# A one-core encoder block: buffer rooms of the last bonus and of the up weights, a second queue for four gate loads, block copies on VectorE, two pinned orders

## The chip, the cores and the metric

The kernel runs on one core of a Trainium2 chip. The core has five engines, each with its own instruction queue. TensorE (PE) multiplies matrices; its weight loads are listed apart as PEld. VectorE (DVE) and ScalarE (ACT) work on rows of elements, and GpSimd (POOL) does a few elementwise operations here. SyncE (SP) does no arithmetic and issues most of the DMA transfers; POOL issues some too. The engines wait for each other and for DMA transfers by semaphores.

The time is the device time of one execution in microseconds (us), as the median of several runs. The profile beside it is of one execution. "Span" is the time from its first instruction to its last.

## The reference

The kernel computes one encoder block in float32, for 1024 positions of 1024 channels. Cut to what matters:

```python
h = rms_norm(x, norm_mix)
proj = h @ w_in                                   # q, k, v | rwkv columns | 2 x 1024 gate columns
attn = windowed_gqa(q, k, v, sink)                # blocks of 128, +-128 positions, softmax with a sink
zr = zr + shift_mu * (centred_shift(zr) - zr)
#   rwkv7_time_mix: r, k, v, two directions d of decay w and rate a
#   state = state * w + (state @ a) b^T + v k^T;   y = state @ r       (a scan over 1024 positions, both ways)
y = (y - mean) * rsqrt(var + eps) * lnx_w + lnx_b # per head of 64 channels
bonus = einsum(rh, k_dir, r_k)[..., None] * vh    # sum over the channels of a head and over d, times v
rw = (y + bonus) * (sigmoid(gl) @ g2)
gates = sigmoid(proj[gate columns])
merged = gates[0] * (attn @ w_up_attn) + gates[1] * (rw @ w_up_rwkv)
x = x + merged @ w_out
x = x + square(relu(rms_norm(x) @ w_ff1)) @ w_ff2
x = x + (p @ w_ple) * sigmoid(rms_norm(x) @ w_ple_gate)
```

## The kernel before

**Precision.** Each float32 operand of the large products is split in two: `split` (lines 196 to 204) casts it on ACT to a matmul type ("hi", line 198), and one subtraction on DVE or POOL makes the rest ("lo", line 199). Each product is then three matmuls, hi by hi, lo by hi and hi by lo (lines 227, 229, 231; 239 to 241 in another helper). So a weight tile goes through a chain before PE can use it: a DMA of 256 KB into a staging tile `wst`, a cast on ACT, a subtraction.

**Rooms.** Tiles come from pools; a tag with `bufs=2` is two rooms that its tiles take in turn. A tile may be written when all that read the former tile of its room is done. Tiles of another pool that has been closed give their bytes to later pools, and there too the new tile waits for the last reader or writer of the old one, even if that is a DMA.

**What sets the order.** A scheduler orders the instructions of each engine by priority and by its own estimates, before the kernel runs. Some are pinned: matmuls of `mmo` and vector instructions of `turn` stay as the program writes them, and `after(x, y)` puts x behind y. On the chip each engine's queue, and each DMA-issuing queue, is worked through in this fixed order: an instruction that waits holds all behind it on the same queue.

**Stages, in the times of the profiled execution.** Up to about 130 us: the first norm and the q, k, v projections. Up to about 280: for four pairs of RWKV heads p = 0 to 3, projections, the two directions (`kd`, `bk`, `ra` and others, written to DRAM for the scan), and the bonus (`add_bonus`, lines 623 to 642): DVE makes the product rk, PE sums it over a head (`px`, lines 619 and 620), PE turns v (`vtp`, line 633) and ACT copies it to `vt`, SP writes `vt` to `v_d`, and DVE multiplies the sum with v into `bv` (line 638), which SP writes to `bv_d`. From about 280 on PE does the gate columns (`gates`, lines 321 to 333, PSUM tile `gmm`; loop m = 0 to 15 over blocks of 128 columns, halves h of 512 positions) while DVE and ACT finish pair 3. Gate m of half 0 needs its weights through `load_w` (lines 206 to 217), two parts of 256 KB each.

336 to 466 us: the attention, eight tiles n of 128 positions. Per tile: scores `sc` on PE (line 934), softmax on DVE and ACT, transposes (`pt`, line 955), the product with v (`po`, line 963) and its way to DRAM. What is left of the gate matmuls of half 0, and gate 0 of half 1, has the lowest priority and fills in between. Beside it runs the inverse of the first block of scan chunks: `low_products` (lines 791 to 816) loads chunk rows `la` and `lb`, multiplies them on PE (`lps`, line 813), and ACT copies them to `lt` (line 815); it does four chunks (NB = 4), all behind tile n = LOW_AT = 3. Then ACT copies the diagonal 32 x 32 blocks to `Lc` (line 823), and DVE inverts them from tile 5 on in about 31 steps (lines 833 and 836) between its softmax work.

481 to 780 us: the scan, 16 steps of 64 positions in each direction (`qps`, `wa`, `ups`, `sps` and so on), pinned in program order. Between a step's matmuls a generator `beside` (line 986) gives PE fill work: the rest of the gates of half 1, then the attention's up-projection (`uaps`) with weights `wust`, split to `wuhi` and `wulo`, and with the activations `gm`, split to `aTh` and `aTl`. For blocks b = 1, 2, 3 of four chunks the inverse is made in the same loop, one block ahead: `low` (line 1272) copies each chunk's diagonal blocks from `lt` to `Lc` on ACT (line 1279, four copies of 32 x 256 elements a chunk, 48 in all), and `inverse_steps` (line 1281) starts on DVE with the transpose `Lp` (line 1285).

735 to 811 us: the two epilogues (group norm: Ln at line 1103, Square at 1109, Exp at 1119 on ACT, with `rwh` and `rwl` as the split results). 811 to 860: the RWKV up-projection (`mmc`, `mmo`), gate by gate: a gate tile `g1t` is loaded from DRAM, DVE scales and adds it, and the sum is split into `mh` and `ml`, which the output projection reads with the weights `wo0h`, `wo0l`. From 860: output projection, norms, the two feed-forward products (`ff1ps`, `ff2ps`) and the last embedding, up to 1684.

## Time and profile before

| what | value |
|---|---|
| median of 3 runs | 1685.11 us (1683.96 to 1685.51) |
| the profiled execution's own time | 1685.89 us |
| its span | 1684.1 us |
| mean granted TensorE clock over the span | 0.986 |
| busy share of the span: PE, DVE, ACT, POOL | 96%, 67%, 50%, 6% |
| 285 to 300 us: span 15.00, PE busy | 10.39 us |
| 330 to 340 us: span 10.00, PE busy | 5.70 us |
| 396 to 420 us: span 24.00, PE busy | 21.10 us |
| 485 to 520 us: span 35.00, PE busy | 31.31 us |
| 690 to 735 us: span 45.00, PE busy | 39.77 us |
| 735 to 811 us: span 76.00, PE busy | 68.35 us |

How the rows are read: a row of the timeline gives the start, the duration, the engine, the source line, the operation, "output<-input", the shape, the count, and in brackets the idle time of the engine just before it with what ended it. Matmul rows overlap, since the next one starts before the former has drained; the chain of waits ("critical") gives them without the overlap. A row of a window gives the busy time of each engine in that stretch, the granted clock (PEclk, 1.00 is full), the busy share of the 16 DMA engines and the GB/s. SPq is SP's issue queue; "DMA x" in the chain is the time until a transfer landed.

### The profile page before, as it was taken

Reading aid. Unit: us, or ns where it says so; the run is one execution under the profiler, and the core shown is the slowest. Engines: PE = TensorE matmul, PEld = TensorE weight load, DVE = VectorE, ACT = ScalarE, POOL = GpSimd, SP = SyncE. Lnnn points to the kernel's source line nnn. Section 1 sums busy time; section 2 is a strip of 40 time slices with the busy share of each in tenths; the row PEclk is TensorE's granted clock in tenths of the full one; section 3 lists DMA queues with packets and bytes.
Section 4 is the critical chain, followed back from the end, with each engine's and each line's share of the span. In section 5 each row is a group of like instructions: output and inputs, shape, how many; then the busy total and the mean of one; then the engine's idle time right before and its main releaser. Section 6 shows DMA issues by size and latency. Waiting matters only on the chain.

```text
span 1684.1 us, 31165 instructions
## 1 busy us (share of the span) xinstructions
PE 1615.9 (96%) x12280; PEld 1307.8 (78%) x12280; DVE 1134.6 (67%) x2055; ACT 844.5 (50%) x1535; POOL 103.1 (6%) x113
## 2 busy tenths in 40 slices
PE   7999998899999999898999999999999999999998
PEld 7987776776677787676778788888888888888887
DVE  5648998265947596777744876667667877685342
ACT  5557887367744545456313554444435344544121
POOL 3440000221200000000000000000000000000000
PEclk9999999999999999799999999999999999999999
DMA  6353556764286554547652154444449865564110
GB/s 223 82 155 98 171 163 202 227 172 130 88 230 198 139 179 134 163 130 238 207 179 100 57 177 161 144 165 147 138 167 349 273 204 162 164 212 148 38 41 38
DMA packets 200834, 269.23 MB, mean 160 GB/s; under 512 B 47728, under 2 KB 103920, under 8 KB 200688
## 3 DMA queue, kind: packets, MB, share of 16 engines
q1 hardware_dynamic: 190752, 254.14, 47.6%
q0 software_dynamic: 9792, 12.59, 2.9%
q8 instruction: 96, 1.57, 0.4%
q10 hardware_dynamic: 144, 0.52, 0.1%
q14 instruction: 50, 0.41, 0.1%
HBM read 186.45 MB, written 80.74 MB: 159 GB/s over the span
## 4 chain that ended last, share of the span: by engine, by line
PE 74%; DVE 10%; DMA 6%; ACT 5%; issue 3%; POOL 1%; SPq 0%; DVEq 0%; ACTq 0%; POOLq 0%
PE ff2ps L1882 18%; PE ff1ps L1630 16%; PE gmm L221 4%; DMA wst<-in_w_col_dram 2%; PE plps L231 2%; PE plps L229 2%; PE plps L227 2%; PE mm L239 2%; PE mm L240 2%; PE mm L241 2%; PE uaps L221 1%; PE gps L221 1%; PE mmo L241 1%; PE mmo L239 1%; PE mmo L240 1%
## 5 line engine op out<-in xcount | busy, mean ns | idle before, releaser
L1882 PE MATMUL ff2ps<-th,sl 128*128 128x512 f32 x448 | 174.3, 389 | 0.0
L1882 PE MATMUL ff2ps<-tl,sh 128*128 128x512 f32 x448 | 174.3, 389 | 0.0
L1882 PE MATMUL ff2ps<-th,sh 128*128 128x512 f32 x448 | 173.9, 389 | 0.0
L198 ACT CAST sh<-sst 128x512 fp32r<-128x512 f32 x109 | 67.8, 622 | 100.4 <-PE ff2ps L1882 50.9
L199 DVE TENSOR_TENSOR sl<-sst,sh 128x512 fp32r<-128x512 f32 x109 | 75.0, 688 | 44.0 <-ACT sh L198 43.5
L1630 PE MATMUL ff1ps<-mh,w1h 128*128 128x512 f32 x256 | 100.3, 392 | 2.0 <-ACT w1h L198 2.0
L198 ACT CAST whi<-wst 128x512 fp32r<-128x512 f32 x100 | 60.3, 618 | 81.9 <-DMA wst<-in_w_col_dram 30.3
L1630 PE MATMUL ff1ps<-ml,w1h 128*128 128x512 f32 x256 | 99.9, 390 | 0.0
L1630 PE MATMUL ff1ps<-mh,w1l 128*128 128x512 f32 x256 | 99.6, 390 | 0.0
L1882 PEld LDWEIGHTS ff2ps<-tl,sh 128*128 128x128 f32 x448 | 84.1, 188 | 17.7 <-DVE tl L199 0.2
L1882 PEld LDWEIGHTS ff2ps<-th,sh 128*128 128x128 f32 x448 | 84.0, 188 | 17.6 <-ACT th L198 0.3
L1882 PEld LDWEIGHTS ff2ps<-th,sl 128*128 128x128 f32 x448 | 84.1, 188 | 17.5
L183 POOL TENSOR_TENSOR rstd<-ms,neghalf 128x1 f32<-128x1 f32 x24 | 14.5, 606 | 1019.7 <-PE ff2ps L1882 572.3
L198 ACT CAST w1h<-w1st 128x512 fp32r<-128x512 f32 x48 | 28.3, 620 | 96.3 <-DMA w1st<-in_w_ff_dram 59.6
L199 DVE TENSOR_TENSOR wlo<-wst,whi 128x512 fp32r<-128x512 f32 x72 | 47.9, 687 | 29.5 <-ACT whi L198 29.4
L199 DVE TENSOR_TENSOR w1l<-w1st,w1h 128x512 fp32r<-128x512 f32 x48 | 31.7, 687 | 51.6 <-ACT w1h L198 51.6
L227 PE MATMUL gmm<-hh,whi 128*128 128x512 f32 x136 | 57.0, 419 | 4.6 <-ACT whi L198 4.6
L1630 PEld LDWEIGHTS ff1ps<-mh,w1h 128*128 128x128 f32 x256 | 48.1, 188 | 12.9 <-ACT w1h L198 2.8
L231 PE MATMUL gmm<-hh,wlo 128*128 128x512 f32 x136 | 56.8, 419 | 0.0
L1630 PEld LDWEIGHTS ff1ps<-mh,w1l 128*128 128x128 f32 x256 | 48.1, 188 | 10.9 <-DVE w1l L199 0.8
L229 PE MATMUL gmm<-hl,whi 128*128 128x512 f32 x136 | 56.5, 416 | 0.0
L1630 PEld LDWEIGHTS ff1ps<-ml,w1h 128*128 128x128 f32 x256 | 48.1, 188 | 10.0
(405 smaller groups left out, 4530.9 us busy)
## 6 DMA issues: line engine op xcount, KB each, us to landing
wst<-in_w_col_dram SPq DMA_DIRECT2D x92, 256.0 KB, 3.4
tst<-in_w_ff_dram SPq DMA_DIRECT2D x80, 256.0 KB, 4.1
w1st<-in_w_ff_dram SPq DMA_DIRECT2D x32, 512.0 KB, 5.1
hid_S<-h SPq DMA_DIRECT2D x64, 256.0 KB, 2.1
sst<-hid_S SPq DMA_DIRECT2D x64, 256.0 KB, 3.2
hid_A<-h SPq DMA_DIRECT2D x48, 256.0 KB, 2.0
sst<-hid_A SPq DMA_DIRECT2D x45, 256.0 KB, 4.0
ra_d<-ra SPq DMA_DIRECT2D x8, 1024.0 KB, 5.7
```

The costliest lines, as they stand in the source:

```text
L183: nc.gpsimd.tensor_tensor(out=r, in0=ms, in1=neghalf.broadcast_to([P, width]), op=ALU.pow)
L198: a = nc.scalar.copy(hi, src)
L199: b = (lo_eng or nc.vector).tensor_tensor(out=lo, in0=src, in1=hi.bitcast(F32), op=ALU.subtract)
L221: tc.keep_in_program_order(nc.tensor.matmul(*a, **kw))
L227: mm(ps, ah, bh, start=(i == 0), stop=False)
L229: mm(ps, ah, bl, start=False, stop=False)
L231: mm(ps, al, bh, start=False, stop=(i == n - 1))
L239: nc.tensor.matmul(ps, ah, bh, start=(i == 0), stop=False)
L240: nc.tensor.matmul(ps, ah, bl, start=False, stop=False)
L241: nc.tensor.matmul(ps, al, bh, start=False, stop=(i == n - 1))
L1630: nc.tensor.matmul(ps, x_[:, k, :], y_[:, k, :], start=start and k + i == 0, stop=k == 3 and i == 2, skip_group_check=True)
L1882: nc.tensor.matmul(banks[bs][i], x_[:, isl], y_, start=fresh and p + j == 0, stop=p == NPR - 1 and j == 2, skip_group_check=True)
```

## The change

1. The four loads of gates m = 1 and 2 of half 0 (two of 256 KB each) are issued from POOL's queue and not SP's (GQ, and the argument q of `load_w`).
2. `bv` of the last pair takes the room of `kd` and no longer that of `vt`.
3. The low products of the first block are made two chunks behind tile 3 and two behind tile 4 of the attention, where all four stood behind tile 3 (LOW_AT).
4. The 48 copies of diagonal blocks in the scan loop are done by DVE in a pinned place, and each chunk's copies one chunk later: those of chunk ci stand ahead of the low products of chunk ci + 1, the last ones ahead of `Lp`. The 4 copies of the first block (line 823) stay on ACT.
5. In the pool of the up-projection, the weights' staging tile for m = 2 and the first gate tile `gta` are allocated and loaded before `wuhi` and `wulo`, so that these take other bytes of the pool.
6. The Exps of the second epilogue are put behind its last Ln, as those of the first already are (EXPIN). In the instruction list the table loads of ACT in the second epilogue go from four to two.
7. The four casts and four subtractions of the output weights `wo0h`, `wo0l` (128 x 1024 each) are put behind the epilogue's last split. They now stand among the instructions of the RWKV up-projection.

```diff
--- before.py
+++ after.py
@@ -35,7 +35,7 @@
 WOAT = (0, 4)
 
 NFS = {0: "s0 c0", 1: "s1 c1 t0", 2: "s2 c2 t1", 3: "s3 c3 t2", 4: "s4 c4 t3", 5: "s5 c5 p0", 6: "s6 c6 p1", 7: "s7 c7 p2"}
-EXPIN = (1, 0)
+EXPIN = (1, 1)
 EPS_AT = (3, 3, 2, 2)
 VH = 8
 TPAT = (1, 3)
@@ -54,6 +54,7 @@
 FILL0 = 4
 
 GATT = 1
+GQ = ((0, 1), (0, 2))
 
 BRIDGE = 6
 FILL = (5, 5, 3, 5, 3, 2, 4, 1)
@@ -65,7 +66,7 @@
 FILLQ = 8
 TURNS = ((0, 0, 4), (3, 2, 5), (3, 2, 5), (4, 3, 1))
 
-LOW_AT = 3
+LOW_AT = (3, 4)
 INV_AT = 5
 GN_EPS = 64e-5
 W_SCALE = -0.5 * float(np.exp(np.float64(-0.5)))
@@ -193,17 +194,20 @@
 
     on_pool = [None]
 
-    def split(hi, lo, src, lo_eng=None, pin=False):
+    def split(hi, lo, src, lo_eng=None, pin=False, behind=None):
 
         a = nc.scalar.copy(hi, src)
         b = (lo_eng or nc.vector).tensor_tensor(out=lo, in0=src, in1=hi.bitcast(F32), op=ALU.subtract)
+        for x_, y_ in zip((a, b), behind or ()):
+            after(x_, y_)
         if lo_eng is nc.gpsimd:
             on_pool[0] = b
         if pin:
             tc.keep_in_program_order(a)
             tc.keep_in_program_order(b)
-
-    def load_w(pl, tag, src, n, bufs=2, sbufs=2, lo_eng=None, stag=None, parts=1, stages=()):
+        return a, b
+
+    def load_w(pl, tag, src, n, bufs=2, sbufs=2, lo_eng=None, stag=None, parts=1, stages=(), q=None):
 
         k = src.shape[1]
         hi = pl.tile([P, k, n], F32R, name="whi", tag=tag + "_hi", bufs=bufs)
@@ -212,7 +216,7 @@
         for i in range(0, k, step):
             spl, stg, sb = stages[(i // step) % len(stages)] if stages else (pl, stag or tag + "_st", sbufs)
             st = spl.tile([P, step, n], F32, name="wst", tag=stg, bufs=sb)
-            nc.sync.dma_start(st, src[:, i:i + step])
+            (q or nc.sync).dma_start(st, src[:, i:i + step])
             split(hi[:, i:i + step], lo[:, i:i + step], st, lo_eng or nc.gpsimd)
         return hi, lo
 
@@ -322,7 +326,7 @@
 
         for m in ms:
             c0 = O_GATE + m * P
-            hi, lo = load_w(PW, "w", w_col(c0), P, parts=2, lo_eng=lo_of(m))
+            hi, lo = load_w(PW, "w", w_col(c0), P, parts=2, lo_eng=lo_of(m), q=nc.gpsimd if (h, m) in GQ else None)
             ps = PMM.tile([P, 512], F32, name="gmm", tag="mm", bufs=2)
             yield from mm3_steps(ps, [(hi[:, k, :], lo[:, k, :], Hh[h][:, k, :], Hl[h][:, k, :]) for k in range(KT)], mm)
             th = PW.tile([P, 512], F32, name="gth", tag="gth", bufs=2)
@@ -633,7 +637,7 @@
                     nc.tensor.transpose(tp[:, j, :], vz[:, (4 * q + j) * P:(4 * q + j + 1) * P], ident)
                 nc.scalar.copy(vt[:, 4 * q:4 * q + 4, :], tp)
             nc.sync.dma_start(v_d[:, p * P:(p + 1) * P].rearrange("(t q) c -> q t c", q=P), vt)
-            bv = A1.tile([P, T], F32, name="bv", tag="vt", bufs=1)
+            bv = A1.tile([P, T], F32, name="bv", tag="kd" if p == NP - 1 else "vt", bufs=1)
             for hs, ps in next(sums):
                 nc.vector.tensor_tensor(out=bv[:, hs], in0=ps, in1=vz[:, hs], op=ALU.mult)
             for e in range(2):
@@ -969,8 +973,10 @@
                 next(low0)
             if n == 1:
                 zi = zi_tile(BI, "zi")
-            if n == LOW_AT:
-                lts[0] = list(low0)[-1]
+            if n in LOW_AT:
+                for _ in range(NB // len(LOW_AT)):
+                    lts[0] = next(low0)
+            if n == LOW_AT[-1]:
                 for d in range(ND):
                     for a in (load_ra(0, d), load_bk(0, d)):
                         after(a, put)
@@ -1009,10 +1015,18 @@
         aTh = UA.tile([P, NP, 512], F32R, name="aTh", tag="aTh", bufs=1)
         aTl = UA.tile([P, NP, 512], F32R, name="aTl", tag="aTl", bufs=1)
 
+        def gate_of(m, h):
+            g = UA.tile([P, 512], F32, name="gta", tag="g1t", bufs=2)
+            nc.sync.dma_start(g, g_d[m, :, 512 * h:512 * h + 512])
+            return g
+
+        sts.append(load_wu(UA, 2))
+        gta = [gate_of(0, 0)]
+
         def weights(m, st=None):
             hi = UA.tile([P, NP, P], F32R, name="wuhi", tag="wu_hi", bufs=3)
             lo = UA.tile([P, NP, P], F32R, name="wulo", tag="wu_lo", bufs=3)
-            split(hi, lo, st or load_wu(UA, m))
+            split(hi, lo, load_wu(UA, m) if st is None else st)
             return hi, lo
 
         def part(k):
@@ -1030,9 +1044,8 @@
             for m in range(KT):
                 hi, lo = ahead.pop(0)
                 if (h, m) != (0, 0) and (h, m) < (1, KT - 1):
-                    ahead.append(weights((m + 1) % KT))
-                g = UA.tile([P, 512], F32, name="gta", tag="g1t", bufs=2)
-                nc.sync.dma_start(g, g_d[m, :, hs])
+                    ahead.append(weights((m + 1) % KT, sts.pop(2) if sts[2:] else None))
+                g = gta.pop() if gta else gate_of(m, h)
                 ps = PMM.tile([P, 512], F32, name="uaps", tag="mm", bufs=2)
                 for j, _ in enumerate(mm3_steps(ps, [(hi[:, k, :], lo[:, k, :], aTh[:, k, :], aTl[:, k, :]) for k in range(NP)], mmo)):
                     if (h, m) == (0, KT - 1) and j and j % 3 == 0:
@@ -1124,7 +1137,7 @@
             ps = PB.tile([P, 2, 256], F32, name="gps2", tag="gps", bufs=2)
             mm(ps, g2[:, p * P:(p + 1) * P], sge, start=True, stop=True)
             nc.vector.scalar_tensor_tensor(out=rs, in0=rs, scalar=col("lnx_b", p), in1=ps, op0=ALU.add, op1=ALU.mult)
-            split(rwh[:, p, :], rwl[:, p, :], rs.rearrange("q a t -> q (a t)"))
+            epi["done"] = split(rwh[:, p, :], rwl[:, p, :], rs.rearrange("q a t -> q (a t)"))
             yield
 
     AC = [PH0, None]
@@ -1271,15 +1284,22 @@
 
     def low(b, ci):
 
-        lt = lts[b] = next(lows[b])
-        if ci == 0:
+        if ci:
+            diagonal(b, ci - 1)
+        else:
             Lcs[b] = BI.tile([P, 32, 32], F32, name="Lc", tag="inv", bufs=3)
+        lts[b] = next(lows[b])
+
+    def diagonal(b, ci):
+
+        lt = lts[b]
         for r0 in range(0, P, 32):
             k = r0 // 32 % 2
-            nc.scalar.copy(Lcs[b][r0:r0 + 32, 8 * ci:8 * ci + 8], lt[r0:r0 + 32, 8 * ci:8 * ci + 8, 32 * k:32 * k + 32])
+            turn(nc.vector.tensor_copy(Lcs[b][r0:r0 + 32, 8 * ci:8 * ci + 8], lt[r0:r0 + 32, 8 * ci:8 * ci + 8, 32 * k:32 * k + 32]))
 
     def inverse_steps(b):
 
+        diagonal(b, NB - 1)
         Lc = Lcs.pop(b)
         Lp = BI.tile([P, 32, 32], F32, name="Lp", tag="inv", bufs=3)
         turn(nc.vector.transpose(out=Lp, in_=Lc.rearrange("s p t -> s t p")))
@@ -1430,7 +1450,7 @@
         for k in ks:
             st = spl.tile([P, 2, 512], F32, name="wst", tag=tag, bufs=sbufs)
             nc.sync.dma_start(st, wov[:, k:k + 2, 512 * n:512 * n + 512])
-            split(wo[n][0][:, k:k + 2], wo[n][1][:, k:k + 2], st)
+            split(wo[n][0][:, k:k + 2], wo[n][1][:, k:k + 2], st, behind=None if n else epi["done"])
 
     wo_tiles(WO1, 0)
 
```

The following rows are from the instruction lists of the engines, in order, with what an instruction waits for in brackets where that is given.

POOL, between the end of the q and k writes and the loads for the attention (`wst` are gate weights, `qT` and `kT` the attention's operands, `wlo` subtractions for gates). Before:

```order
L754 DMA qT<-qT_d 128x1024
L767 DMA qT<-qT_d 128x1024
L762 DMA kT<-kT_d 128x4x256
L199 TENSOR_TENSOR wlo<-wst,whi 128x512 x2
L762 DMA kT<-kT_d 128x4x256 x2
L199 TENSOR_TENSOR wlo<-wst,whi 128x512 x2
L762 DMA kT<-kT_d 128x4x256
```

After:

```order
L219 DMA wst<-in_w_col_dram 128x512 x2
L758 DMA qT<-qT_d 128x1024
L219 DMA wst<-in_w_col_dram 128x512
L771 DMA qT<-qT_d 128x1024
L219 DMA wst<-in_w_col_dram 128x512
L766 DMA kT<-kT_d 128x4x256
L200 TENSOR_TENSOR wlo<-wst,whi 128x512 x2
L766 DMA kT<-kT_d 128x4x256 x2
```

Three of the four new loads stand ahead of a `qT` load, and all four ahead of the first `kT` load.

DVE, from the end of the last pair to the attention's first softmax (`s2l` and `wlo` are subtractions, `smk` the masked scores). Before:

```order
L199 TENSOR_TENSOR wlo_2871<-wst_2872,whi_2870 128x512 [waits DMAHW5_49,PE_49,Activation_49]
L199 TENSOR_TENSOR wlo_2871<-wst_2876,whi_2870 128x512 [waits DMAHW0_49,Activation_49]
L638 TENSOR_TENSOR bv_3027<-px_3028,z_2693 128x512 [waits DMAHW2_49,DMAHW4_49,PE_49,Activation_49]
L638 TENSOR_TENSOR bv_3027<-px_3031,z_2693 128x512 [waits PE_49]
L917 TENSOR_SCALAR nsink_3060<-band_2922 128x8 [waits DMAHW7_49,DVE_49]
L935 ISA smk_3066,mx_3062<-sc_3067,band_2922 128x256 [waits DMAHW6_49,PE_49]
```

After:

```order
L200 TENSOR_TENSOR s2l_3010<-rk_2595,s2h_3009 128x512 [waits Activation_49]
L200 TENSOR_TENSOR wlo_2871<-wst_2876,whi_2870 128x512 [waits DMAHW2_49,Activation_49]
L642 TENSOR_TENSOR bv_3027<-px_3028,z_2693 128x512 [waits PE_49]
L642 TENSOR_TENSOR bv_3027<-px_3031,z_2693 128x512 [waits PE_49]
L921 TENSOR_SCALAR nsink_3060<-band_2922 128x8 [waits DMAHW3_49,DVE_49]
L939 ISA smk_3066,mx_3062<-sc_3067,band_2922 128x256 [waits PE_49]
```

The first `bv` waited for two DMA queues, PE and ACT; it now waits for PE alone.

ACT, where the up-projection's first weights are cast in the scan (`gth` is the last gate of half 1, `W` belongs to a scan step). Before:

```order
L329 ACTIVATE gth_8291<-gmm_8076 128x512 [waits DMAHW7_49,PE_49,Activation_49]
L1216 COPY W_8368<-wa_8333 128x512 [waits DVE_49,PE_49]
L198 CAST wuhi_8304<-wust_4673 128x512 [waits DMAHW5_49,Activation_49]
L198 CAST aTh_8302<-gm0_4612 128x512 x2
L198 CAST aTh_8302<-gm1_4613 128x512 x2
L198 CAST wuhi_8320<-wust_4675 128x512
```

After:

```order
L333 ACTIVATE gth_8291<-gmm_8076 128x512 [waits DMAHW3_49,PE_49,Activation_49]
L1229 COPY W_8372<-wa_8337 128x512 [waits DVE_49,PE_49]
L199 CAST wuhi_8308<-wust_4673 128x512
L199 CAST aTh_8302<-gm0_4612 128x512 [waits Activation_49]
L199 CAST aTh_8302<-gm0_4612 128x512
L199 CAST aTh_8302<-gm1_4613 128x512 x2
```

The first `wuhi` waited for a DMA queue and for ACT; it now waits for nothing.

## The prediction

> **What bounds the kernel now.** I read the page first, then windows by stage, then the timeline and the chain of waits in the windows that have gaps.
>
> ```profile
> PE 1615.9 (96%) x12280; PEld 1307.8 (78%) x12280; DVE 1134.6 (67%) x2055; ACT 844.5 (50%) x1535; POOL 103.1 (6%) x113
> 285.00:300.00 15.00, 10.39 (x38) 7.86 (x36) 9.38 (x10) 4.21 (x6) 0.76 (x1) 0.77 0.97 304
> 300.00:330.00 30.00, 30.00 (x130) 24.16 (x129) 6.90 (x9) 10.76 (x19) 9.34 (x9) 1.00 0.78 228
> 330.00:340.00 10.00, 5.70 (x21) 4.30 (x21) 2.24 (x7) 1.73 (x3) 3.14 (x3) 0.87 0.76 234
> 396.00:420.00 24.00, 21.10 (x212) 15.09 (x213) 9.30 (x34) 16.38 (x38) 4.14 (x5) 0.93 0.57 155
> 420.00:466.00 46.00, 41.85 (x216) 28.29 (x213) 44.62 (x148) 33.23 (x93) 8.56 (x7) 0.97 0.26 81
> 860.00:960.00 100.00, 99.54 (x464) 81.23 (x463) 59.84 (x90) 37.10 (x63) 5.68 (x8) 1.00 0.28 101
> ```
>
> The columns are span, then PE, PEld, DVE, ACT and POOL busy, the granted clock, the DMA share, and GB/s. PE sets the time: 96% busy over the span, 99.54 of 100 us from 860 on, where nothing changes. So there is nothing to win except PE's gaps and the slow clock behind them, and the change works in windows that have both. The gaps of the windows quoted up to 466 us are 4.6, 0, 4.3, 2.9 and 4.2 us.
>
> **Part 1, gate loads on POOL's queue.**
>
> ```profile
> 280.44 4.16 SPq L640 DMA_DIRECT2D bv_d<-bv  x2
> 284.69 8.75 DMA wst<-in_w_col_dram
> 279.62 0.56 POOL L754 DMA_DIRECT2D qT<-qT_d  x1 [162.43 <-PE px L221]
> 294.14 0.80 PE L227 MATMUL gmm<-hh,whi 128*128 128x512 f32 x1 [4.61 <-ACT whi L198]
> 298.67 0.43 PE gmm L227
> 301.09 0.23 PE gmm L229
> wst<-in_w_col_dram SPq DMA_DIRECT2D x92, 256.0 KB, 3.4
> ```
>
> SP was held from 280.44 to 284.6 by the writes of an earlier `bv`; only then did it issue the next gate's weights, which took 8.75 us to land against a median of 3.4, with the DMA engines 0.97 busy. PE idled 4.61 us and then ran some 13 matmuls at 0.43 in place of 0.23, that is 13 x 0.20 = 2.6 us. POOL was issuing a load at 279.62, so its queue could have issued these weights about 5 us earlier (284.69 - 279.62), more than the 4.61 us missing. Ceiling 7.2 us. Floor: the bytes in flight are the same, and if the DMA engines and not the queue set the 8.75 us, the start 5 us earlier still brings something; floor 2. I take 5.2, nearer the ceiling, because SP's hold (4.2 us) alone is nearly the 4.61 missing. All four loads come ahead of the first `kT` on POOL, whose loads begin at 279.62; the scores that need it come at 336.40, so even 20 us of delay there are free.
>
> The Trainium skill, "Trainium Kernel Development and Optimization", section Key Constraints, says that DMAs of SP, ACT and POOL run on the same 16 DMA engines and that issuing from several only saves the sequencer's issue time. Read strictly this is worth only SP's own hold: 284.69 - 280.44 = 4.2 us earlier, about 4 us of the 7.2. It does not speak of the case here, where a queue stands behind an instruction that waits. The sum goes by the rows.
>
> **Part 2, room of the last `bv`.**
>
> ```profile
> 327.03 0.39 PE L620 MATMUL px<-s2l,one_r 128*128 128x512 f32 x1
> 331.02 4.50 DMA v_d<-vt
> 335.65 1.29 DVE L638 TENSOR_TENSOR bv<-px,z 128x512 f32<-128x512 f32 x2 [22.38 <-DMA v_d<-vt]
> 336.40 0.74 PE L934 MATMUL sc<-kT,qT 128*128 128x256 f32 x4 [4.30 <-DVE bv L638]
> 339.86 0.43 PE gmm L229
> ```
>
> The sums `px` are there at 327.4, but `bv` stands until 335.65, until the write of `vt` to DRAM has landed, because it takes that room. The scores wait 4.30 us for it, since they take the PSUM rooms of `px`. In the new list `bv` waits for PE alone. Its new room, `kd`, was last read when rk was made, which is ahead of `px` in any case. The scores can start about 327.4 + 0.7 + 0.1 = 328.2. Gained: the gap 4.30 and 8 matmuls at 0.43 (8 x 0.20 = 1.6 us), 5.9 us. `bv_d` is written earlier, which nobody waits for before the epilogue. Gate matmuls that stood ahead of the scores (15 fewer in the new PE list before the first one) move behind them; they are fill work and lose nothing as long as their weights are there. Bounds: 7 with what later reading gives, and 3 if the weights of the gates are the next to be late (DMA share 0.76 to 0.78). I take 6.
>
> **Part 3, low products in two halves.**
>
> ```profile
> 403.39 4.88 DMA lb<-bk_d
> 408.36 0.30 PE L813 MATMUL lps<-lb,la 64*64 64x64 f32 x2 [2.54 <-DMA lb<-bk_d]
> 396.38 2.79 PE L963 MATMUL po<-pT,V 128*64 128x512 f32 x12
> 419.38 2.80 PE L963 MATMUL po<-pT,V 128*64 128x512 f32 x12 [0.24 <-ACT pT L959]
> ```
>
> Products of four chunks in a row behind tile 3 use up their loaded rows; the third waits 2.54 us for a load, then, as behind the other gaps, a few matmuls run slow (six would be 1.2 us). Tile 3 to tile 4 takes 23.0 us (419.38 - 396.38). With two chunks, a tile, and two more, the loads of chunks 2 and 3 have a tile's time. Gain up to 2.54 + 1.2 + 2 for the smoother tile = 6; nothing if the inverse on DVE (44.62 of 46 us busy from 420 to 466) is what ends the stage, since `Lp` then starts no earlier. `Lc` stays on ACT there. I take 4: parts 1 and 2 bring everything earlier by the same amount, and the start of `Lp` with them. The attention stage gets 28 gate matmuls less (6.5 us) and its tail 28 more; the tail waits for the end of the inverse on DVE anyway. I book 0 for that: it may cost 3 if the weights of these 28 come late, half of their 6.5, or win 2 of the 4.2 that PE idles from 420 to 466.
>
> **Part 4, diagonal copies on DVE.**
>
> ```profile
> 498.10 1.65 ACT L1279 COPY Lc<-lt 32x256 f32<-32x256 f32 x4
> 507.72 0.33 PE L221 MATMUL lps<-lb,la 64*64 64x64 f32 x2 [1.66 <-ACT lt L815]
> 510.99 0.32 PE L221 MATMUL lps<-lb,la 64*64 64x64 f32 x2 [1.41 <-ACT lt L815]
> 515.28 2.04 DVE L1285 STREAM_TRANSPOSE Lp<-Lc 128x1024 f32<-128x1024 f32 x1 [5.96 <-ACT Lc L1279]
> 706.28 0.68 DVE L864 COPY zi<-Zn 32x1024 f32<-32x1024 f32 x1
> 520.00:552.00 32.00, 31.97 (x691) 26.08 (x689) 30.66 (x78) 13.58 (x26) 0.00 (x0) 1.00 0.64 181
> ```
>
> On ACT four copies take 1.65 us and stand between a chunk's `lt` and the next; PE waits 1.66 and 1.41 us for `lt` here, and DVE 5.96 us for the last `Lc`. DVE copies 1024 elements on 32 partitions in 0.68 us; no row has 256. Bounds for one: 0.68 x 256/1024 = 0.17, and ACT's 0.41. I take 0.25, nearer the scaled one, so 48 copies are 12 us on DVE, 36 of them in a place where it waits anyway. PE wins up to 1.66 + 1.41 at step 0, and a little at steps 4 and 8; but where the inverse runs DVE is 30.66 of 32 us busy, and PE's gap there is 0.03. I take 3 (0 to 5).
>
> **Part 5, rooms of the up weights.**
>
> ```profile
> 684.72 4.11 DMA g_d<-gth
> 688.91 0.62 ACT L198 CAST wuhi<-wust 128x512 fp32r<-128x512 f32 x1 [2.85 <-DMA g_d<-gth]
> 689.56 0.69 DVE L199 TENSOR_TENSOR wulo<-wust,wuhi 128x512 fp32r<-128x512 f32 x1 [4.14 <-ACT wuhi L198]
> 690.10 0.80 PE L221 MATMUL uaps<-aTh,wuhi 128*128 128x512 f32 x1 [3.74 <-ACT aTh L198]
> 704.64 3.62 PE L221 MATMUL qps<-Zn,lt 32*32 32x32 f32 x128 [4.30 <-DVE Zn L1300]
> ```
>
> `wuhi` takes bytes of a gate tile `gth` whose write to DRAM lands at 688.83. In the new list it waits for nothing and can follow ACT's instruction before it, 2.85 us earlier, which is ACT's idle time in the row. PE's first gap shrinks by that; DVE, which stands 4.14 us, goes on with the inverse as much earlier, and the second gap ends with DVE's `Zn`. So the stretch from 686 to 704.64 gets 2.85 us shorter, and part of the slow clock goes: eight `uaps` at 0.43 (1.6 us). I take 4 (2 to 6).
>
> **Parts 6 and 7, epilogue and output weights.**
>
> ```profile
> 788.37 1.28 ACT L1103 ACT_TABLE_LOAD   x1
> 794.54 1.28 ACT L1119 ACT_TABLE_LOAD   x1
> 792.51 0.50 PE L221 MATMUL mups<-rwh,one_r 128*128 128x512 f32 x1 [2.38 <-ACT rwh L198]
> 790.25 1.04 ACT L198 CAST wo0h<-wst 128x1024 fp32r<-128x1024 f32 x1
> 791.32 1.23 DVE L199 TENSOR_TENSOR wo0l<-wst,wo0h 128x1024 fp32r<-128x1024 f32 x1 [0.52 <-ACT wo0h L198]
> 855.68 0.50 PE L239 MATMUL mmo<-wo0h,mh 128*128 128x512 f32 x1 [1.25 <-ACT mh L198]
> ```
>
> Two of four table loads go (2 x 1.28 = 2.56 us of ACT), and a cast of 1.04 leaves the chain that ends with PE's wait of 2.38 us: 3 us there. The casts come back in the RWKV up-projection: 4 x 1.04 on ACT and 4 x 1.23 on DVE, in the queue ahead of `mh` and `ml`. That stage's chain goes through DVE and ACT and PE waits 1.25 us at its end. Price: 0 if they fit where DVE waits for loads, up to 4.9 of DVE. I take 1.5, so +1.5 (-2 to +3.5) for both.
>
> The Trainium skill, "ScalarE: Activation LUTs", section What ACT_TABLE_LOAD costs, gives about 2.66 us for a switch, of which 1.28 is the load and the rest a drain; by that two would be 5.3 us of ACT. The rows agree on 1.28. They show no drain of that size: 788.37 + 2.66 would be 791.03, and ACT casts at 790.25. The sum goes by 1.28.
>
> **Sum.** 5.2 + 6 + 4 + 0 + 3 + 4 + 1.5 = 23.7 us. The profiled execution took 1685.89 (span 1684.1 and 1.8 around it): 1662.2. The median, 1685.11, lies 0.8 below it, so 1661.4; I say 1662.
>
> **The rivals.**
>
> *The gates' weights become the bound in place of the waits removed.* For: DMA share 0.97 and 0.78 from 285 to 330. With both gaps gone PE asks 7 us earlier for the later gates' weights, and two staging rooms give a gate's load, cast and subtraction (3.4, the median, + 0.62 + 0.69, the rows of the same shape in part 5 = 4.7 us for each half) little more time than its 24 matmuls take (24 x 0.23 = 5.5). Against: 30.00 of 30 us busy from 300 to 330 with the same loop. It would leave 2 of part 1, 3 of part 2, and 2 of part 3: 2 + 3 + 2 + 3 + 4 + 1.5 = 15.5, so 1670.
>
> *DVE becomes the bound.* For: DVE 97% busy from 420 to 466 and 96% from 520 to 552. Then part 3 gives 0, part 4 costs 3 (12 of its copies at 0.25 inside the busy stretches), and the moved subtractions cost 2 more than booked: 23.7 - 4 - 6 - 2 = 11.7, so 1674.
>
> *Slower: SP's queue holds the scan.* The new early loads of part 5 (`wust` for m = 2 and `gta`) need rooms of a pool that opens late. If these rooms come free late, SP stands with the loads of `la`, `lb` and the scan rows behind it. Price of one such hold: a load's 4.88 us plus the slow clock behind it, 2.6, so 7.5 us a step. It makes the kernel slower from the fourth step on (4 x 7.5 = 30, over 23.7 + 3.4): 1692. Against: both loads stand at one place of the queue, ahead of the first `wuhi`, so one hold is likelier than four.
>
> *The change doesn't do what it says in the rooms.* Bytes of parts 2 and 5 could wait for another late transfer. The lists show no DMA wait at either instruction, so only a PE or ACT wait can remain. It would take 6 + 4: 1672.
>
> **How the numbers follow.** Forecast 0.60; weights 0.17; DVE 0.10; rooms 0.05; slower 0.04; all gains near their ceilings 0.04 (7.2 + 7 + 6 + 2 + 5 + 6 + 3.5 = 36.7, so 1649). About 0.2% (3.4 us) is the least that a measurement of this kernel can tell from no change. Faster by more than that holds in all but the slower rival and in the tails of the DVE and weights cases, which take 0.04: faster 0.90, same 0.05, slower 0.05. The likeliest case alone spans 1655 to 1669; the range reaches down half way to the ceilings and up beyond the DVE case, 1652 to 1679.
>
> **What would show it.** Right: no PE gap over 1 us from 285 to 300 and from 327 to 337; `bv` within 1.5 us of the last `px`; `lps` with no wait for a load; the first `uaps` within 1 us of `W`; two table loads in the second epilogue. Wrong: `gmm` waiting for `whi` in new places (weights), `qps` or `lps` waiting for DVE more than before (DVE), `la` or `lb` late at several steps (SP's queue), or PE gaps of over 2 us each ahead of `mmo` (output weights).

## The result, and where the time went

| | kernel before | changed kernel | ratio, 95% interval |
|---|---|---|---|
| first session, median | 1685.28 us (8 runs, 1683.4 to 1687.87) | 1676.01 us (8 runs, 1670.11 to 1681.76) | 0.9944 [0.9923, 0.9965] |
| another session, median | 1684.68 us (12 runs) | 1675.65 us (7 runs) | 0.9944 [0.9924, 0.9965] |

The change makes the kernel 9.3 us faster (0.56%). The forecast was 1662, some 23 us faster, with a range of 1652 to 1679. The way was right and the range holds the time, but the gain is well under half of what was forecast; that the range reached up to the time was for the sake of another case (DVE as the bound), and its holding is luck. Single runs of either kernel spread by some 10 us (the changed kernel's over 11.7 in the first session, those of the kernel before over 9.8 in the other); the last section comes back to that.

The profiled execution of the changed kernel took 1677.74 us, span 1676.0, to be held against 1685.89 and 1684.1. Its windows, with the columns as in the prediction:

```profile
285.00:300.00 15.00, 13.72 (x58) 10.39 (x58) 10.71 (x12) 8.56 (x12) 1.31 (x2) 1.00 0.89 292
300.00:330.00 30.00, 27.46 (x116) 21.55 (x115) 9.64 (x16) 9.05 (x16) 9.86 (x9) 0.94 0.88 250
330.00:340.00 10.00, 8.45 (x44) 6.61 (x42) 3.97 (x20) 4.98 (x18) 6.30 (x6) 1.00 0.97 292
396.00:420.00 24.00, 23.47 (x178) 16.20 (x180) 16.99 (x60) 22.13 (x59) 1.70 (x3) 1.00 0.43 126
466.00:485.00 19.00, 10.48 (x172) 8.69 (x163) 2.91 (x5) 5.23 (x9) 0.00 (x0) 0.64 0.85 251
```

The gaps that the prediction spoke of have shrunk: 1.3 us from 285 to 300 (4.6 before), 1.6 from 330 to 340 (4.3), 0.5 from 396 to 420 (2.9). From 300 to 330, where PE had no gap, it now has one of 2.5. The last row is new. The same window of the kernel before was nearly full:

```profile
466.00:485.00 19.00, 17.76 (x251) 12.85 (x248) 9.91 (x14) 6.65 (x12) 0.00 (x0) 0.97 0.93 257
```

So PE lost 8.5 us and a third of its clock at the place where the attention ends and the scan begins. The starts of a few matmuls, read from PE's timeline, turn this into a ledger. The second profile of the changed kernel is from the other session.

| PE starts | before | changed | changed, second profile | gained since the row above (before minus changed) |
|---|---|---|---|---|
| last `px` | 327.03 | 325.34 | 325.79 | 1.7 |
| first `po` (tile 0) | 357.96 | 347.61 | 347.70 | 8.7, of which 4.0 are 17 gate matmuls moved behind |
| last `po` (tile 7) | 465.62 | 449.41 | 449.50 | 5.9, of which 2.6 are 11 more gate matmuls |
| first `qps` | 481.29 | 479.67 | 479.08 | -14.6, of which 6.6 are these 28 gate matmuls |
| `qps` of the third block inverse | 704.64 | 696.58 | 691.13 | 6.4 |
| first `mmc` | 802.32 | 792.34 | 786.95 | 1.9 |
| first `mmo` | 849.47 | 841.41 | 835.00 | -1.9 |
| end of the span | 1684.1 | 1676.0 | 1669.2 | 0.0 |

Without the moved matmuls (0.235 us each) the stages up to the attention's end gained 9.6 us, its tail lost 8.0, the scan gained 6.4, and the rest nothing. The scan's figure is that of one execution: by the second profile it gained 11.3 (212.05 us from the first `qps` to that of the third inverse, against 216.91 and 223.35). Here is the tail in the changed kernel, SP's timeline first:

```profile
454.35 0.33 SPq L219 DMA_DIRECT2D wst<-in_w_col_dram  x1
461.67 1.63 SPq L797 DMA_DIRECT2D la<-ra_d  x1
465.42 1.99 SPq L1001 DMA_DIRECT2D gm<-at_d  x4
467.46 0.91 SPq L1005 DMA_DIRECT2D wust<-in_w_up_attn_dram  x2
468.46 0.85 SPq L219 DMA_DIRECT2D wst<-in_w_col_dram  x2
```

Then its chain of waits, DVE and PE (the `gm` on DVE is the scan's masked product; the `gm` that SP loads is the attention's activation):

```profile
468.46 5.72 DMA wst<-in_w_col_dram
474.85 0.69 DVE L200 TENSOR_TENSOR wlo<-wst,whi 128x512 fp32r<-128x512 f32 x1 [9.37 <-ACT whi L199]
475.46 1.02 DVE L1181 TENSOR_TENSOR gm<-gps,gmask 128x384 f32<-128x384 f32 x2
476.07 1.97 PE L1198 MATMUL tmps<-ident,bkc 128*128 128x128 f32 x8 [8.52 <-DVE gm L1181]
```

Gate m = 1 of the second half needs two weight loads. SP issued the first at 454.35. The second stands behind 22 other loads, sixteen for the scan, four `gm` and two `wust`, and left at 468.46. SP's rows show it issuing these for some 12 of the 14.1 us, so the queue was busy rather than held by a wait. On DVE the subtraction `wlo` that needs it stands ahead of the mask product `gm`, and PE's `tmps` waits for that. One late load thus held three queues. In the kernel before, both loads of this gate (457.90) and both of the next (469.54) stood ahead of the scan's loads on SP:

```profile
457.90 1.71 SPq L215 DMA_DIRECT2D wst<-in_w_col_dram  x2
469.54 1.06 SPq L215 DMA_DIRECT2D wst<-in_w_col_dram  x2
471.14 0.95 SPq L898 DMA_DIRECT2D bkc<-bk_d  x2
477.06 1.35 PE L221 MATMUL gps<-rac,bkc 64*64 64x128 f32 x32 [1.21 <-DVE gm L1168]
```

The gap there was 1.21 us, by the same path and behind the later pair, so the pattern could have been read before the change. Why the scheduler, which orders by its own estimates, placed the loads differently in the changed kernel is not shown.

### The profile page after: what moved, and what is told of

The parts are those of the page before. It is cut to its first block, busy times and chain, and to the rows that moved or that the text cites. A ratio compares the mean times of both kernels' runs of the same rounds, so it can differ in the third digit from the quotient of the medians.

```text
span 1676.0 us, 31183 instructions
## 1 busy us (share of the span) xinstructions
PE 1611.0 (96%) x12280; PEld 1305.8 (78%) x12280; DVE 1156.0 (69%) x2103; ACT 821.1 (49%) x1485; POOL 105.4 (6%) x117
## 4 chain that ended last, share of the span: by engine, by line
PE 71%; DVE 13%; DMA 7%; ACT 3%; issue 3%; SPq 1%; POOL 1%; DVEq 0%; POOLq 0%; ACTq 0%
PE ff2ps L1902 18%; PE ff1ps L1650 16%; DMA wst<-in_w_col_dram 3%; PE gmm L225 2%; PE mm L243 2%; PE mm L244 2%; PE mm L245 2%; PE plps L235 2%; PE plps L233 2%; PE plps L231 2%; DMA g1t<-g_d 2%; DVE tmp L1313 1%; DVE Z L1316 1%; PE qps L225 1%; PE mmo L245 1%
```

## The experiments

All times are medians; the ratio is to the kernel before, run in the same session on the same chip (1682.3 to 1684.7 in these sessions). As base for the single parts serves the first experiment, in which the tail's wait is gone, so that a part's worth is not hidden by it. "Above the base" compares medians of different sessions, between which the kernel before moved by up to 2.4 us.

**The tail's weights on another queue.** One edit to the changed kernel:

```diff
-GQ = ((0, 1), (0, 2))
+GQ = ((0, 1), (0, 2), (1, 1))
```

> The changed kernel, and besides it the two weight loads of gate m = 1 of the second half go by GpSimd's queue. The first gap of the scan in the changed kernel is 8.52 us ahead of tmps (476.07); DVE stands on a wlo there, whose weights SP issued at 468.46 behind la, lb, gm and wust. Theory A (SP's queue makes them late): they leave at about 455, the gap ahead of tmps falls below 1.5 us, the slow clock behind it goes (about 4 us), time 1663 to 1667. Theory B (the DMA engines are full there, 0.81 to 0.86 busy, and the bytes cannot come sooner): the gap stays over 5 us, time 1673 to 1678.

Measured: 1669.67 us, ratio 0.9918 [0.9891, 0.9944]. POOL's timeline and PE's `tmps`:

```profile
453.74 0.57 POOL L219 DMA_DIRECT2D wst<-in_w_col_dram  x1 [0.30 <-POOL wlo L200]
455.95 0.56 POOL L219 DMA_DIRECT2D wst<-in_w_col_dram  x1 [0.30 <-POOL wlo L200]
466.93 1.03 PE L1198 MATMUL tmps<-ident,bkc 128*128 128x128 f32 x8
```

The second load leaves 12.5 us earlier (455.95 against 468.46), `tmps` runs without a wait, and the first `qps` comes at 468.82 against 479.67. The DMA engines were not the limit. Theory A holds at the place, but the time stays above its 1663 to 1667: of the 10.9 us gained there it shows some 6, as the repetition in one session confirms:

> The changed kernel itself, beside the next two runs on the same chip. 8 to 11 us faster than the kernel before; the gap ahead of the first tmps 7 to 9 us.

> The changed kernel with the loads of the second half's gate m = 1 on GpSimd's queue, again. Theory A (the wait at the start of the scan and the slow clock behind it cost the changed kernel its 8 to 11 us of landmark, of which later stages keep more than half): 4 to 8 us faster than the changed kernel in the same session. Theory B (the later stages take it back, since the inverse on DVE sets the end of the third block): within 2 us of it.

Measured: the changed kernel 1675.65 us, 0.9944 [0.9924, 0.9965], its gap ahead of `tmps` 8.15; with the edit 1669.35 us, 0.9921 [0.9894, 0.9949]. The medians differ by 6.3 us. The intervals still overlap, so the time alone would not prove the edit; the wait that is gone in both profiles does. Some of the gain is given back between the third inverse's `qps` and the first `mmc`, which takes 95.8 us in both profiles of the changed kernel and 100.9 and 97.6 with the edit; why stays open.

**The first three parts alone, and the other four alone.** Made from the changed kernel by setting the other parts back: the first with ACT's copies, the old order in the up-projection's pool, EXPIN = (1, 0) and no `behind`; the second with

```diff
-GQ = ((0, 1), (0, 2))
+GQ = ()
-LOW_AT = (3, 4)
+LOW_AT = (3,)
-            bv = A1.tile([P, T], F32, name="bv", tag="kd" if p == NP - 1 else "vt", bufs=1)
+            bv = A1.tile([P, T], F32, name="bv", tag="vt", bufs=1)
```

> Parts 1, 2 and 3 alone (gate loads on POOL, room of bv, low products in two halves); parts 4 to 7 as before. Theory A (what the attention wins is given back at the start of the scan): the last po comes at 449 to 451, qps at 479 to 481, and the slow clock behind the gap costs 3 to 4 us more: 1682 to 1688, no gain. Theory B (the loss sits in parts 4 to 7): the 9 us that the attention wins are kept, 1674 to 1677.

> Parts 4 to 7 alone; parts 1 to 3 as before, so the attention and the start of the scan are as before (qps at 481). Theory A: the scan wins 6.4 us and the 3.7 that the slow clock took in the changed kernel, the epilogue and the RWKV up-projection cancel: 1673 to 1677. Theory B (parts 4 to 7 lose, parts 1 to 3 win): 1682 to 1687.

Measured: parts 1 to 3 alone 1680.68 us, 0.9985 [0.9969, 1.0002]; parts 4 to 7 alone 1679.48 us, 0.9975 [0.996, 0.999]. Theory A is right on the first by its places (last `po` at 449.37, a wait of 8.79 us ahead of `tmps`, `qps` at 479.90), though the time is 1.3 us under its range. On the second the gain is 3 to 4 us, less than theory A said and not the loss of theory B. The profiles hold a surprise. From the first `qps` to that of the third inverse the kernel before took 223.35 us, parts 4 to 7 alone 217.24 (698.02 - 480.78), and parts 1 to 3 alone 216.12 (696.02 - 479.90), though they change nothing in the scan. ACT's rows of parts 1 to 3 alone tell why:

```profile
679.53 0.59 ACT L1228 COPY W<-wa 128x512 f32<-128x512 f32 x1 [0.73 <-PE wa L225]
680.01 0.62 ACT L199 CAST wuhi<-wust 128x512 fp32r<-128x512 f32 x1
```

`wuhi` follows `W` at once, where in the kernel before it waited 2.85 us for the write of the last gate. In the instruction list with parts 1 to 3 (not shown here) it waits for the write of the gate before the last: which of two rooms the last gate takes has flipped. So the removal of this wait, which was to be the gain of part 5, came with parts 1 to 3 as well, and was counted once too often.

**Part 1 undone on the base**, GQ = ((1, 1),):

> As the run with the two loads of the second half on GpSimd's queue, but without part 1 (the four loads of the first half are back on SP's queue). Theory A (the weights are bound by bytes and by two staging rooms there, so the queue is worth little: px moved by 1.7 us): 1 to 2.5 us slower than with part 1. Theory B (part 1 is worth the 5.2 us that the prediction gave it): 4.5 to 6 us slower.

Measured: 1671.9 us, 0.9927 [0.9901, 0.9954], 2.2 us above the base, in theory A's range, though the two intervals overlap. PE's gap is back, while with part 1 the changed kernel has two smaller ones. The row of this experiment:

```profile
293.20 0.80 PE L231 MATMUL gmm<-hh,whi 128*128 128x512 f32 x1 [4.05 <-ACT whi L199]
```

The rows of the changed kernel, POOL, the chain of waits, and PE:

```profile
279.45 0.56 POOL L219 DMA_DIRECT2D wst<-in_w_col_dram  x1 [12.46 <-PE px L225]
289.01 0.55 POOL L219 DMA_DIRECT2D wst<-in_w_col_dram  x1 [7.02 <-DVE wlo L200]
279.45 7.89 DMA wst<-in_w_col_dram
289.01 5.35 DMA wst<-in_w_col_dram
293.14 0.50 PE L235 MATMUL gmm<-hh,wlo 128*128 128x512 f32 x1 [1.14 <-DVE wlo L200]
307.06 0.53 PE L231 MATMUL gmm<-hh,whi 128*128 128x512 f32 x1 [2.48 <-ACT whi L199]
```

The load did leave 5.2 us earlier (279.45 against 284.69) and landed 6.1 us earlier. Then the next load stood 7.02 us on POOL until DVE had freed its staging room. The queue was not the limit for long: it is the ring of load, cast, subtraction and room, at a DMA share of 0.89. The windows from 285 to 330 us say the same: of 45 us PE is busy 40.4 in the kernel before and 41.2 in the changed one.

**Part 2 undone on the base** (`tag="vt"` for every pair):

> As the run with the loads of the second half's gate m = 1 on GpSimd's queue (1669.7 us, the base of this and the next three), but part 2 undone: the last bv is back in vt's room. Theory A (part 2 is worth what the prediction gave it, and nothing behind it takes it back): scores about 6 us later against px, qps 4 to 6 us later than 468.8, time 1674 to 1676. Theory B (the inverse on DVE or the weights absorb it): qps within 2 us, time 1668 to 1671.

Measured: 1677.77 us, 0.9969 [0.9958, 0.998], 8.1 us above the base, clear of its interval and 1.8 above theory A's range; first `qps` at 475.57. A `qps` by itself says little: in the nine profiles of the base and of kernels that differ from it only behind this point, it starts anywhere from 468.8 to 474.5. Counted from the last `px` it is steadier, 144.2 to 146.9 us, and here 150.2: 3 to 6 us at the place. The old wait is back as it was:

```profile
333.53 1.29 DVE L642 TENSOR_TENSOR bv<-px,z 128x512 f32<-128x512 f32 x2 [24.69 <-DMA v_d<-vt]
334.28 0.74 PE L938 MATMUL sc<-kT,qT 128*128 128x256 f32 x4 [3.79 <-DVE bv L642]
```

**Part 3 undone on the base** (LOW_AT = (3,)):

> The base with part 3 undone: all four low products behind tile 3. Theory A (booked 4 us): lps waits 2.5 us for lb again and the last po and qps come 3 to 4 us later, 1672 to 1674. Theory B (the inverse on DVE ends the stage): the gap at lps is there but qps comes within 1.5 us of 468.8, 1668 to 1671.

Measured: 1673.97 us, 0.9948 [0.9928, 0.9969], 4.3 us above the base, in theory A's range, though the intervals overlap; first `qps` at 474.53, 149.6 us behind the last `px`. From the last `px` to the last `po` it takes 130.8 us, where the kernels with parts 1 to 3 take 123.7 to 126.2. So the part's worth is seen at its place. The wait for the load is only 1.49 us here, so most of it lies elsewhere in the tiles:

```profile
397.60 0.30 PE L817 MATMUL lps<-lb,la 64*64 64x64 f32 x2 [1.49 <-DMA lb<-bk_d]
```

**Part 4 undone on the base** (copies on ACT, each chunk's own; of the edit only the copy is shown, the order of the calls is set back too):

```diff
-            turn(nc.vector.tensor_copy(Lcs[b][r0:r0 + 32, 8 * ci:8 * ci + 8], lt[...]))
+            nc.scalar.copy(Lcs[b][r0:r0 + 32, 8 * ci:8 * ci + 8], lt[...])
```

> The base with part 4 undone: the diagonal copies on ACT. Theory A (DVE is the bound where the inverse runs: twelve copies in a row take 3.56 us there ahead of Lp, as long as DVE's wait for ACT had been, 4.06): Lp of the third inverse 166.5 to 168.5 us behind the first qps, as with the copies on DVE (167.6), time within 2 us, 1668 to 1672. Theory B (the prediction's 3 us): Lp 2 to 3 us later, 1672 to 1674.

Measured: 1672.58 us, 0.9941 [0.9928, 0.9954], 2.9 us above the base, but its first `qps` comes at 474.54, 5.7 us later than the base's though nothing ahead of it differs; from there to the third inverse's `qps` it takes 217.72 us against the base's 217.01. `Lp` of the third inverse comes 169.06 us behind the first `qps` (base 167.56). The base's second profile has 213.89 and 164.97 for these two stretches, so they can't tell 1 or 2 us. The time falls in theory B's range and `Lp` between the theories: what part 4 is worth stays open. What the copies do is seen where they stand. In the changed kernel, and with ACT's copies (parts 1 to 3 alone):

```profile
644.10 3.57 DVE L1298 COPY Lc<-lt 32x256 f32<-32x256 f32 x12
647.70 1.98 DVE L1305 STREAM_TRANSPOSE Lp<-Lc 128x1024 f32<-128x1024 f32 x1
696.58 3.63 PE L225 MATMUL qps<-Zn,lt 32*32 32x32 f32 x128 [6.02 <-DVE Zn L1320]
```

```profile
647.45 2.00 DVE L1302 STREAM_TRANSPOSE Lp<-Lc 128x1024 f32<-128x1024 f32 x1 [4.06 <-ACT Lc L1296]
696.02 3.63 PE L225 MATMUL qps<-Zn,lt 32*32 32x32 f32 x128 [5.62 <-DVE Zn L1317]
```

DVE's wait for ACT (4.06 us) has become DVE's own twelve copies (3.57 us, 0.30 each), and `Lp` starts at the same time. PE waits 6 us for the end of this inverse in both.

**Part 5 undone on the base** (the weights' staging tile and `gta` allocated as before):

> The base with part 5 undone: wuhi back in its old room of the pool. Theory A (with parts 1 to 3 the first wuhi falls on the room of the gate before the last, whose write has long landed, so the wait is gone without part 5): first uaps within 1 us of W, time 1668 to 1671. Theory B (the prediction's 4 us): uaps waits 3.7 us for the write of the last gate again, 1672 to 1675.

Measured: 1670.64 us, 0.9926 [0.9906, 0.9946], 1.0 us above the base: theory A. The wait is not there without part 5:

```profile
672.16 0.59 ACT L1228 COPY W<-wa 128x512 f32<-128x512 f32 x1 [0.78 <-PE wa L225]
672.65 0.62 ACT L199 CAST wuhi<-wust 128x512 fp32r<-128x512 f32 x1
```

**Parts 6 and 7 undone on the base**, EXPIN = (1, 0), and `behind=None`:

> The base (the run with the loads of the second half's gate m = 1 on GpSimd's queue, 1669.7 us) with part 6 undone: the second epilogue has its four table loads again. Theory A (the prediction's 2.56 us): the waits of the second epilogue's mups for rwh and rwl sum to 2 to 3 us more than the base's 4.1 (0.56, 0.31, 1.32, 0.53, 1.69, less what is under 0.25), time 1671.5 to 1673.5. Theory B (ACT has slack there): within 1 us, 1668 to 1671.

> The base with part 7 undone: the casts and subtractions of wo0 stand in the epilogue again. Theory A (the prediction's balance: the epilogue wins about 1, the RWKV up-projection loses 1 to 2): from the first mmc to the first mmo 46 to 47.5 us, as in the kernel before (47.15), where the kernels with part 7 have 46.4 to 49.1; the time within 2 us of the base. Theory B (the moved work is on the chain of ml): 3 us shorter there and 2 to 3 us faster, 1666 to 1668.

Measured: without part 6 1671.72 us, 0.9927 [0.9905, 0.9949], 2.1 us above the base, which is inside what the runs tell apart; the waits ahead of the second epilogue's `mups` sum to 4.8 us against the base's 4.6, so the time is near theory A and the place near theory B, and this stays open. Without part 7 1666.54 us, 0.9898 [0.9881, 0.9915], 3.1 us below the base: theory B by the time, with intervals that overlap. The place shows only a part of it. From the first `mmc` to the first `mmo` the thirteen profiles with part 7 take 46.4 to 49.4 us, 48.2 on average, and the four without it 46.7 to 47.7, 47.2 on average. In the changed kernel the moved work stands here, on DVE:

```profile
799.73 2.36 DVE L200 TENSOR_TENSOR wo0l<-wst,wo0h 128x1024 fp32r<-128x1024 f32 x2 [0.26 <-ACT wo0h L199]
806.22 2.35 DVE L200 TENSOR_TENSOR wo0l<-wst,wo0h 128x1024 fp32r<-128x1024 f32 x2
```

and PE waits 1.08 us at 811.33 for DVE's `g1t` and 1.49 at 820.82 for ACT's `mh`, the latter a wait that the kernel before did not have. The base, which has part 7 too, has neither of the two in its first profile.

**The rest of SP's queue.** On the base, the second half's `gm` loads on POOL:

```diff
-                nc.sync.dma_start(epi["at"][k], at_d[:, k, 512 * h:512 * h + 512])
+                (nc.gpsimd if h else nc.sync).dma_start(epi["at"][k], at_d[:, k, 512 * h:512 * h + 512])
```

> The base with the second half's attention loads (gm) on GpSimd's queue too. In the base they wait on SP for the aTl subtractions and hold the up weights wust behind them; these leave at 673.14 and land at 679.3, and DVE stands 1.76 us on the wulo that needs them, in the middle of the third inverse. Theory A (SP's queue holds the loads): wust leaves 3 to 5 us earlier against the first wuhi, DVE's wait falls under 0.5 us, Zn and qps come 1 to 1.8 us earlier, 1667.5 to 1669. Theory B (the room of wust, freed by DVE, is what holds them): no change, 1669 to 1671.

and beside it three `wulo` subtractions on POOL (`nc.gpsimd` as `lo_eng` where the staging tile is one of the early three):

> As the run before, and the first three wulo subtractions on GpSimd instead of DVE, which has nothing else to do there. Theory A (the third inverse on DVE sets the gap of 6.58 us ahead of qps): three times 0.69 us leave DVE's chain, qps 2 us earlier and the slow clock a little shorter, 1665 to 1667.5; PE waits up to 0.6 us more at the first uaps, since GpSimd takes 1.3 us for one. Theory B (the scan's matmuls set it): no change against the run before.

Measured: 1667.11 us, 0.9902 [0.9885, 0.9918], and 1669.43 us, 0.9914 [0.9889, 0.9938]. In the first the wait of DVE is gone as theory A says. The base, then the experiment, the same subtraction:

```profile
680.06 0.69 DVE L200 TENSOR_TENSOR wulo<-wust,wuhi 128x512 fp32r<-128x512 f32 x1 [1.76 <-ACT wuhi L199]
```

```profile
674.82 0.68 DVE L200 TENSOR_TENSOR wulo<-wust,wuhi 128x512 fp32r<-128x512 f32 x1
```

PE's wait for `Zn` falls from 6.58 us to 4.72, and the time by 2.6 us, less than the intervals tell. That the edit is what shortened the wait for `Zn` isn't shown by this: the base without part 5 has these loads on SP and waits 4.71 us there. The subtractions on POOL bring nothing to the time, as theory B says; PE's wait for `Zn` stays (4.71) and new ones come ahead of it (0.89 for `aTl`, 2.23 for the mask product).

**All three together** (gate m = 1 and `gm` on POOL, part 7 undone):

> The loads of gate m = 1 and of the second half's gm on GpSimd's queue, and part 7 undone. Theory A (the three add up: 4 to 8, 2.6 and 3 us): 9 to 13 us faster than the changed kernel, 1663 to 1666 where the kernel before has 1683. Theory B (the same slack twice): no faster than the run with part 7 undone alone was, 17 us below the kernel before.

Measured: 1669.14 us, 0.9913 [0.9889, 0.9937]. Theory B: no faster than one of them with the base. The lowest median of all is the base without part 7 (1666.54 us, 0.9898), 9 us under the changed kernel. Whether that kernel is truly better than the base, the runs can't tell: the intervals overlap, and adding the `gm` loads to it did not help.

## Why the prediction was wrong

The forecast summed 15.2 us up to the start of the scan (parts 1, 2 and 3), 7 in the scan (4 and 5) and 1.5 behind it. The ledger says 1.6, 6.4 and 0. The scan's sum came out near in this profile (11.3 in the second); the first one fell, for two reasons.

*The step that failed most is the sentence on the tail, "I book 0 for that".* The 28 gate matmuls that move behind the last `po` were taken as free fill, with a bound of 3 us if their weights came late. They did run as fill: PE has no wait from the last `po` to 467.5 us. Late was a weight load of the gate that stands behind them, and the wait for it cost 8.0 us net (8.52 of wait, and slow clock behind it). Nor does the tail wait for the end of the inverse on DVE, as the prediction had it: in the kernel before, `Zn` is done by 467.1 us, 14 us ahead of the first `qps`. What I had not done is to read SP's list past the last attention tile: it has the second weight load of gate m = 1 behind the scan's loads, `gm` and `wust`. The bound was half of the moved matmuls' own time, but a late load is priced by the wait of the queues behind it, not by the work that it delays. The mechanism stood in the text in another place: the slower rival held that SP's queue could hold the scan's loads, one hold at 7.5 us. It was the other way round, the scan's loads held the weights, once, at 8.5.

*Part 1 was sized wrong:* 5.2 booked, 1 to 2 measured (1.7 by the ledger's `px`, 2.2 by undoing it; over all profiles the last `px` starts at 325.5 on average with part 1 and at 326.5 without). The load left 5.2 us earlier, as computed, but PE's gap moved to 307 us. Its floor in the prediction was 2. This is the first rival, the gates' weights as the bound in place of the wait, at part 1 alone; it was given 0.17. The Trainium skill, "Trainium Kernel Development and Optimization", section Key Constraints, has it that the queues share the same 16 DMA engines and that issuing from several only saves the time to issue; by that I had put part 1 at 4 us. For this place the trace goes the Trainium skill's way and further, since rooms, too, set the pace (7.02 us). In the tail, too, it is the time to issue that is saved, but that was long: the move of two loads to POOL is worth 6.3 us there, because it takes them out from behind 22 others that SP needed some 12 us to issue, at a DMA share of 0.85.

*Part 2:* 6 booked; `sc` behind `px` by 1.4 us where it was 9.4, and 8.1 us by undoing it, of which 3 to 6 are seen up to the first `qps`. The mechanism is right, with the first `bv` no longer waiting, and so is the size as far as the runs can tell.

*Part 3:* 4 booked, 4.3 by undoing it, 3.3 in the ledger (5.9 less 2.6). Right, though the wait for `lb` itself was the smaller part. That DVE's inverse would absorb it did not happen: counted from the last `px`, the last `po` and the first `qps` moved.

*Part 4:* 3 booked; 2.9 by undoing it, with intervals that overlap and landmarks that can't tell. The copies cost 0.30 each, not 0.25, and at the third inverse they replaced DVE's wait by as much work of its own. This is the second rival (DVE as the bound) at that one place: PE waits 6 us for `Zn` with the copies on either engine.

*Part 5:* 4 booked, 1.0 by undoing it. The wait is gone; but parts 1 to 3 removed it too, by flipping the rooms of the last gates. The sum took each part against the kernel before, and the two share one wait.

*Parts 6 and 7:* +1.5 booked, 0 in the ledger: 1.9 won in the epilogue, 1.9 lost in the up-projection. Two table loads did go. The price of the moved output weights was the larger: undoing part 7 gives 3.1 us by the time, of which the trace places 1.0 in the stage where they now stand; where the rest is stays open. On the drain of 1.38 us that the Trainium skill, "ScalarE: Activation LUTs", section What ACT_TABLE_LOAD costs, adds to a load: undoing part 6 costs 2.1 us with an interval of some 4, which supports neither 2.56 nor 5.3.

The parts' worths on the base (2.2, 8.1, 4.3, 2.9, 1.0, 2.1 and -3.1) sum to 17.5 where the base is 13.8 below the kernel before; with an uncertainty of some 2 us on each that is no contradiction, and single figures shouldn't be read closer.

Of the prediction's signs of being right, `bv` beside the last `px` (325.31), the `lps` without a wait and the two table loads came. A PE gap of 1.14 us at 293 stayed, and the first `uaps` starts 1.67 us behind `W`, not within 1; the wait for `whi` at 307 is its sign for the gates' weights. Two of its small sums don't come out: 2.54 + 1.2 + 2 is 5.7, not 6, and 1 less twice 0.04 is 0.92, not 0.90. Nothing above hangs on either.

## What to carry to other kernels

When a stage is made shorter, read the issuing queue's list at the stage's end, not only at the places that the change names: a scheduler that works by its own estimates puts the next loads in another order, and one load behind a dozen others costs its whole wait on every engine that is behind it. Price a late load by the wait, with the slow clock behind it, never by the work that it feeds. And when several parts of a change each remove a wait, ask for each whether it still stands once the others are in.

## What the runs showed of the hardware that I had not expected

The spread of the runs goes with the clock. In the first session the changed kernel's fastest run (1670.11 us) had a mean granted clock of 0.994, its slowest (1681.76) 0.988; the kernel before in the other session had 0.988 at 1679.89 and 0.985 at 1689.72. Two profiled executions of the changed kernel, 1677.74 and 1670.94 us, agree within 0.6 us in every landmark up to the first `qps` (the wait ahead of `tmps` is 8.52 and 8.15 us). Behind the same wait the clock stays low for very different times. The first, then the second:

```profile
470.00:480.00 10.00, 3.93 (x24) 3.09 (x26) 2.91 (x5) 2.92 (x5) 0.00 (x0) 0.56 0.77 249
480.00:490.00 10.00, 10.00 (x199) 8.55 (x196) 0.61 (x2) 2.89 (x5) 0.00 (x0) 0.59 0.85 239
560.00:570.00 10.00, 7.12 (x152) 5.76 (x145) 1.77 (x4) 1.90 (x5) 1.10 (x2) 0.67 0.34 100
```

```profile
470.00:480.00 10.00, 4.22 (x70) 3.67 (x72) 2.92 (x5) 2.92 (x5) 0.00 (x0) 0.66 0.80 264
480.00:490.00 10.00, 9.20 (x256) 7.44 (x251) 3.34 (x6) 4.73 (x8) 0.00 (x0) 1.00 0.88 263
560.00:570.00 10.00, 10.00 (x227) 7.68 (x217) 4.03 (x11) 3.14 (x7) 0.00 (x0) 0.83 0.40 107
```

Summed over all windows of 10 us, one minus the granted clock times the window's length is 18.8 us in the first and 11.6 in the second: a difference of 7.2, where the spans differ by 6.8 (1676.0 and 1669.2). A gap of 2.88 us ahead of a `wy` (PE's timeline has that matmul at 563.88 and at 559.63) was followed by a low clock in both, 0.67 and 0.83 in the window at 560. The Trainium skill, "TensorE: Matmul & The Clock Gate", Part 1, gives an idle window of some 3.4 us before the clock falls, free-running. That would let the length of the slow stretch depend on where in the window a gap falls, and agrees with the two stretches behind `tmps`; but the gap of 2.88 us is shorter than that window, so the figure does not hold here as a threshold. In the kernel before, the gap of 2.54 us ahead of `lps` (408.36) was followed by a granted clock of 0.50 from 409 to 412 us. This kernel has some 10 us of spread in its time, and a part worth 2 us can't be timed by six runs; stretches between landmarks ahead of the first gap are steadier (144.2 to 146.9 us from the last `px` to the first `qps` in nine profiles).

The `qps` of the inverses shows how much a wait costs beyond itself. The same 128 small matmuls of the changed kernel, in PE's timeline, where no wait stands ahead of them:

```profile
623.97 2.21 PE L225 MATMUL qps<-Zn,lt 32*32 32x32 f32 x128
```

Behind the wait of 6.02 us (the row at 696.58, above) they took 3.63 us, at a granted clock of 0.50 from 696.0 to 700.5: 1.42 us more for the same work, on top of the wait.
